# Another layout of the slots in which a DeltaNet mixer emits its work

## The chip, the cores and the metric

The kernel runs on one core of one Trainium2 chip. A core has five engines that run side by side and wait for each other on semaphores: TensorE (PE, matrix products; its weight loads are shown apart as PEld), VectorE (DVE), ScalarE (ACT), GpSimd (POOL) and SyncE (SP, which here only starts transfers). Transfers between the core's memory and the chip's main memory are made by 16 DMA engines. Each engine takes its instructions in one fixed order. The metric is the device time of one execution in microseconds; less is better.

## The reference, cut to what matters

One inference step of a small trunk of two layers on 128 context tokens and 512 latent tokens of width 1024. Layer 0 mixes tokens with a gated DeltaNet, layer 1 with a long convolution (Hyena); each is followed by a SwiGLU feed-forward. The change concerns the DeltaNet mixer alone.

```python
def _gdn_mixer(h, w_in, conv_w, a_log, dt_bias, onorm, w_out, s0):
    proj = h @ w_in
    qkv = jax.nn.silu(_dwconv(proj[..., :GDN_CONV_W], conv_w)).astype(f32)
    q = _l2norm(...) * GDN_DK ** -0.5
    k = _l2norm(...)
    v = ...
    gate = proj[..., GDN_CONV_W:GDN_CONV_W + GDN_V_W]...
    o_f, s_f = _chunk_gated_delta(q, k, v, g[:, :, 0], beta[:, :, 0], s0[:, 0])
    o_b, s_b = _chunk_gated_delta(rev(q), rev(k), rev(v), ...)
    o = o_f + rev(o_b)
    o = (o * lax.rsqrt(jnp.mean(o * o, axis=-1, keepdims=True) + EPS)
         * onorm.astype(f32) * jax.nn.silu(gate))
    return o.reshape(...) @ w_out, jnp.stack([s_f, s_b], axis=1)
```

Inside `_chunk_gated_delta`, chunks of 64 tokens are prepared independently of each other (a triangular system is solved for each), and then a scan over the chunks carries a 128x128 state: two chunks for the context, eight for the latent tokens, in both directions.

## The kernel before

All 640 tokens lie together, features on the partitions. Dense products are made with each operand split into a high and a low part (three matmuls of 320 columns for each block of 128 features), so one head's projection of one kind is 2 halves x 8 blocks x 3 = 48 matmuls.

The mixer (`gdn`) is written as generators that yield after each part of their work. For each head there are these streams:

- `gemm` (`gdn_gemm`, L940 and after), one for each of q, k and v (numbers 0, 1, 2; `GEMM_ORDER` takes k first): a 512 KB weight load, its split on ACT and DVE, 48 matmuls `ps_p` in 9 parts, copies to `xp`. `conv` (`gdn_conv`) follows: the short convolution, five steps of 0.9 us on DVE and ACT, in 6 parts.
- `pre` (`gdn_pre` and `gdn_norms`, L979 to L1122), 18 parts: transposes, sums of squares on ACT, a reciprocal root on DVE, `fa` (L1053), then a trip through main memory. The ACT queue sends `fa` out (`ft`, L1060) and brings 16x16 blocks back (`ln`, L1067); DVE negates them into `bn` (L1073, L1074) and solves small triangular systems in many short operations. The results go out and back again (L1112, L1119) as `tm` and `tt`.
- `chunks` (`gdn_chunks`, L1125 to L1184), 11 parts: the rest of the solve, 50 matmuls of 64 to 128 columns (`ps_c`, `ps_aq`, `ps_y`), and the transposed v in `vyz`.
- `scan` (`gdn_scan`, L1187 to L1262), 30 parts, ten steps: PE `ps_s` (L1214), DVE `y` (L1219), PE (L1225 or L1227), ACT `w` or `od` (L1233), PE (L1248), DVE `s` (L1254), for both directions side by side.
- `norm` (`gdn_norm`), 4 parts: the output's norm and its transpose. `gate` (`gdn_gate`), 9 parts: the gate's projection, 48 matmuls `ps_gate` with a weight load and a split like those of `gemm`; its result is stored to main memory. `finish` (`gdn_finish`): a finished head is loaded, multiplied by its gate where that was not done yet, and split into the high and low parts (`xh`, `xl`, L316, L317) that the output product `ps_o` reads.
- `loads`: parts of `ada` (L192 to L226), the products that give the modulation of later sublayers. Two parts make one step: two 512 KB loads and four matmuls `ps_ada` of 32 rows, each in its own quarter of the array. There are 64 parts, that is 32 steps, in the mixer.

The loop over heads has 11 iterations, h from -3 to 7. Iteration h emits the scan of head h, the chunks of head h+1, the preparation of head h+2, the projections and convolutions of head h+3 and the norm of head h-1. So the first three iterations fill the pipeline (the ramp), in h = 5, 6, 7 the projections have run out, and at h = 7 the loop drains. Each iteration has 30 slots, and `weave` walks through them: in slot t a stream with n parts and slots (a, b) emits parts until n(t+1-a)/(b-a) are out. Within one slot the streams come in the order of `EMIT`.

```python
        for t in range(slots):
            for st in live:
                g, n, a, b, done = st
                while st[4] < min(n, n * (t + 1 - a) / (b - a)):
                    next(g, None)
                    st[4] += 1
```

`PERIOD` holds the slots of the streams that every head has; where it has three entries, the first is for the ramp, the second for h = 0 to 4, the third for h = 5 and later. `GATES[g]` gives the iteration and the slots of gate g. `LOADS[h+3]` gives the number of `ada` parts of iteration h and their slots. The framework below then orders the instructions of each engine: an instruction that is emitted earlier goes first where both are ready by the framework's own estimate of times. So the place of a part is a rank, not a fixed time.

Weight loads and `ada` loads share five buffers (`raw`) and the SP queue. The DMAs of `ft` and `ln` go by the ACT queue.

Of the kernel before, what the change touches and what calls it, by code (L numbers as in the profile page):

```python
# [33 lines left out]
SLOTS = 30  # L34
PERIOD = dict(
    scan=(0, SLOTS),
    norm=(11, 21),
    pre=((2, 21), (1, 25), (4, 25)),
    chunks=((7, 30), (1, 25), (3, 20)),
    gemm=((2, 8, 14), (0, 10, 20), (22, 0, 11)),  # L40
    gemm_len=(8, 7, 10),
    finish=(27, 30),
)
GEMM_ORDER = (1, 0, 2)

GATES = (
    (5, 15, 25),
    (-3, 17, 20),
    (6, 16, 24),
    (4, 5, 14),  # L50
    (4, 13, 28),
    (3, 23, 30),
    (7, 27, 30),
    (7, 3, 15),
)

LOADS = (
    (0, 0, 28),
    (3, 10, 26),
    (0, 5, 30),  # L60
    (10, 3, 26),
    (3, 1, 22),
    (1, 7, 29),
    (3, 6, 30),
    (6, 0, 26),
    (13, 0, 21),
    (18, 0, 24),
    (11, 5, 30),
)

EMIT = ['scan', 'loads', 'norm', 'conv', 'chunks', 'pre', 'gemm', 'finish', 'gate']
MOD_PARTS = (4, 5, 4, 1, 1, 0, 1, 3, 4)
HALVES = (slice(0, 320), slice(320, 640))
DIAG = 128 * 128 + 128
# [13 lines left out]
class _Kernel:  # L88
# [624 lines left out]
    def gdn(self, xs):  # L713
        nc, A, V, G, PE, I = self.nc, self.A, self.V, self.G, self.PE, self.I
        W = I["gdn_w_in"][0]
        with ExitStack() as st:
# [78 lines left out]
            for h in range(-3, H):  # L795
# [3 lines left out]
                def add(name, stream, n, slots):  # L799
                    streams.append((EMIT.index(name), stream, n, *slots))  # L800

# [887 lines left out]
```

## Time and profile before

| | us |
|---|---|
| three runs | 2103.25, 2105.75, 2108.15; median 2105.75 |
| the profiled execution's own time | 2103.4 |
| its span in the profile | 2101.6 |
| PE busy in the span | 2033.6 (97%) |
| DVE, ACT, POOL busy | 1260.7, 794.1, 135.6 |
| granted TensorE clock, mean | 0.989 |
| mixer, first projection matmul to first matmul of the output product | 135.1 to 715.1 |

The span runs from the first to the last instruction of the profile. "Busy" of PE is the time in which at least one matmul is under way; matmuls overlap, and their ends are modelled, so a busy PE may still have room. The granted clock is the share of full speed that TensorE's throttle let through. The ramp lies at 135 to 268 us, and the iterations h = 0 to 7 begin, by the second part of each scan, at about 268, 310, 371, 424, 482, 556, 615 and 677 us; the last scan ends at 714.

### The profile page before, as it was taken

The page shows a single profiled execution, that of the slowest core. Times are in us where ns is not written, and L with a number is a line of the kernel's source. Part 1 is how long each engine was busy: PE and PEld are TensorE (multiplying, and loading weights), DVE is VectorE, ACT ScalarE, POOL GpSimd, SP SyncE. Part 2 cuts the span into 40 slices and gives each one's busy share as a digit, 9 for nine tenths or more (in the row PEclk, how much of TensorE's full clock was granted, in tenths as well). Part 3 has the DMA queues.
Part 4 walks back from the last instruction along what each step waited for, and adds up shares of the span by engine and source line. Part 5 has one row for each costly group of instructions (what it writes and reads, how often), then busy time and mean ns, then how long its engine had stood idle before and what let it go on. Part 6 is the DMA issues. An engine that isn't in the chain of part 4 may idle for free.

```text
span 2101.6 us, 34710 instructions
## 1 busy us (share of the span) xinstructions
PE 2033.6 (97%) x13779; PEld 1889.1 (90%) x13779; DVE 1260.7 (60%) x2649; ACT 794.1 (38%) x1761; POOL 135.6 (6%) x241
## 2 busy tenths in 40 slices
PE   7998999999989999999999999999999999999997
PEld 4677888988866899999999999999889999999997
DVE  6887887876654464434434467878775443443444
ACT  4456445555533443212222243333344321221222
POOL 0131011110110100000000001010000000000000
PEclk8999999999989999999999999999999999999998
DMA  7856453344555632222222253222453222222221
GB/s 236 274 184 154 113 153 100 83 124 115 183 180 181 200 119 62 79 81 70 72 81 71 58 162 100 82 85 76 141 161 95 72 81 71 71 81 71 71 63 58
DMA packets 344833, 237.01 MB, mean 113 GB/s; under 512 B 62274, under 2 KB 314810, under 8 KB 344671
## 3 DMA queue, kind: packets, MB, share of 16 engines
q1 hardware_dynamic: 322495, 230.18, 36.7%
q10 hardware_dynamic: 22176, 4.62, 1.1%
q8 instruction: 108, 1.77, 0.4%
q14 instruction: 54, 0.44, 0.1%
HBM read 202.57 MB, written 32.19 MB: 112 GB/s over the span
## 4 chain that ended last, share of the span: by engine, by line
PE 81%; DVE 7%; ACT 4%; DMA 3%; issue 2%; POOL 0%; ACTq 0%; POOLq 0%; DVEq 0%
PE ps_g L131 15%; PE ps_u L131 15%; PE ps_d L131 15%; PE ps_hp L143 8%; PE ps_o L131 5%; PE ps_p L143 4%; PE ps_ada L209 2%; PE ps_ab L1467 2%; PE ps_g L1524 2%; PE ps_gate L143 1%; PE ps_s L1248 1%; PE ps_s L1214 1%; PE ps_y L1161 1%; PE ps_s L1225 1%; DMA ft<-fa 1%
## 5 line engine op out<-in xcount | busy, mean ns | idle before, releaser
L118 ACT CAST wh<-raw 128x1024 fp32r<-128x1024 f32 (+2 forms) x241 | 220.8, 921 | 461.3 <-PE ps_d L131 199.3
L119 DVE TENSOR_TENSOR wl<-raw,wh 128x1024 fp32r<-128x1024 f32 (+2 forms) x241 | 257.2, 1071 | 79.1 <-ACT wh L118 78.1
L131 PE MATMUL ps_g<-fh,wh 128*128 128x320 f32 (+1 forms) x704 | 220.2, 313 | 0.0
L131 PE MATMUL ps_g<-fh,wl 128*128 128x320 f32 (+1 forms) x704 | 219.6, 312 | 0.0
L131 PE MATMUL ps_u<-fh,wh 128*128 128x320 f32 (+1 forms) x704 | 219.5, 312 | 0.0
L131 PE MATMUL ps_u<-fh,wl 128*128 128x320 f32 (+1 forms) x704 | 219.4, 312 | 0.0
L131 PE MATMUL ps_g<-fl,wh 128*128 128x320 f32 (+1 forms) x704 | 218.0, 310 | 0.0
L131 PE MATMUL ps_u<-fl,wh 128*128 128x320 f32 (+1 forms) x704 | 217.9, 310 | 0.0
L416 DVE SCALAR_TENSOR_TENSOR x<-ps_d,mod,x 128x128 f32<-128x128 f32 x144 | 58.8, 437 | 154.0 <-PE ps_d L131 153.9
L131 PEld LDWEIGHTS ps_g<-fl,wh 128*128 128x128 f32 x704 | 133.6, 190 | 0.4 <-DVE fl L308 0.2
L131 PEld LDWEIGHTS ps_g<-fh,wh 128*128 128x128 f32 x704 | 133.5, 190 | 0.3 <-ACT fh L307 0.2
L131 PEld LDWEIGHTS ps_u<-fh,wh 128*128 128x128 f32 x704 | 133.6, 190 | 0.0
L131 PEld LDWEIGHTS ps_u<-fl,wh 128*128 128x128 f32 x704 | 133.4, 190 | 0.0
L131 PEld LDWEIGHTS ps_u<-fh,wl 128*128 128x128 f32 x704 | 132.8, 189 | 0.0
L131 PEld LDWEIGHTS ps_g<-fh,wl 128*128 128x128 f32 x704 | 132.5, 188 | 0.0
L143 PE MATMUL ps_p<-xh,wh 128*128 128x320 f32 x384 | 128.4, 334 | 1.8 <-ACT junk L1000 0.9
L143 PE MATMUL ps_hp<-xh,wh 128*128 128x322 f32 (+1 forms) x384 | 123.0, 321 | 0.7 <-DVE xp L1415 0.7
L143 PE MATMUL ps_p<-xh,wl 128*128 128x320 f32 x384 | 122.5, 319 | 0.0
L143 PE MATMUL ps_p<-xl,wh 128*128 128x320 f32 x384 | 122.2, 318 | 0.0
L143 PE MATMUL ps_hp<-xh,wl 128*128 128x320 f32 (+1 forms) x384 | 119.5, 311 | 0.0
L143 PE MATMUL ps_hp<-xl,wh 128*128 128x320 f32 (+1 forms) x384 | 119.4, 311 | 0.0
L131 PE MATMUL ps_d<-xh,wl 128*128 128x320 f32 x384 | 118.8, 309 | 0.0
(376 smaller groups left out, 5110.7 us busy)
## 6 DMA issues: line engine op xcount, KB each, us to landing
raw<-in_ada_w_dram SPq DMA_DIRECT2D x96, 512.0 KB
raw<-in_ffn_w_gu_dram SPq DMA_DIRECT2D x88, 512.0 KB
raw<-in_gdn_w_in_dram SPq DMA_DIRECT2D x33, 512.0 KB
raw<-in_ffn_w_down_dram SPq DMA_DIRECT2D x32, 512.0 KB
raw<-in_hy_w_in_dram SPq DMA_DIRECT2D x24, 512.0 KB
h_lat<-hlo SPq DMA_DIRECT2D x16, 512.0 KB
hs<-h_lat SPq DMA_DIRECT2D x32, 256.0 KB
raw<-in_ffn_w_down_dram SPq DMA_DIRECT2D x16, 384.0 KB
```

The source lines that it names most:

```text
L118: self.A.copy(wh[:, ks, :], v[:, ks])
L119: self.V.tensor_sub(wl[:, ks, :], v[:, ks], wh[:, ks, :])
L131: self.PE.matmul(ps, a[:, k, :], b[:, sl], start=(n == 0), stop=(n == 3 * nk - 1))
L143: self.PE.matmul(ps, a[:, k, :], b[:, sl], start=(n == 0), stop=(n == 3 * nk - 1))
L209: PE.matmul(ps[32 * j : 32 * j + 32, :], self.sc[:, k, :], loaded[j * 512 // n][:, c : c + 512], start=(k == 0), stop=(k == KD - 1), skip_ ...
L416: V.scalar_tensor_tensor(out=x[d][:, sl], in0=p1[:, pl], scalar=gate[:, c, d : d + 1], in1=x[d][:, sl], op0=ALU.mult, op1=ALU.add)
L1161: PE.matmul(ps[:, n : n + 128], tm[:, d, t, :], cur[:, d, t, :], start=True, stop=True)
L1214: PE.matmul(pss[d][:, 0:128], qk[:, t, c * 128 : c * 128 + 128], state[seq, d], start=True, stop=True)
L1225: PE.matmul(p2, lt[:, d, t, c, :], ys[d], start=True, stop=True)
L1248: PE.matmul(pss[d][:, 256:384], ktok[:, t, c, :], ws[d], start=True, stop=True)
L1467: PE.matmul(ps, a_[:, m, it, js], b_[it], start=(c == 0), stop=(c == 5))
L1524: PE.matmul(pv[:, gi * 256 : gi * 256 + 256], a_[:, e, cs], b_[:, m, jt, :], start=(c == 0), stop=(c == 11))
```

## The change

Only constants change. No instruction is added to the program or taken from it; the streams are emitted in other slots, and in another order within a slot.

```diff
 PERIOD = dict(
     scan=(0, SLOTS),
-    norm=(11, 21),
-    pre=((2, 21), (1, 25), (4, 25)),
+    norm=(12, 19),
+    pre=((2, 21), (0, 24), (0, 25)),
     chunks=((7, 30), (1, 25), (3, 20)),
-    gemm=((2, 8, 14), (0, 10, 20), (22, 0, 11)),
-    gemm_len=(8, 7, 10),
-    finish=(27, 30),
+    gemm=((1, 8, 14), (0, 10, 20), (22, 1, 11)),
+    gemm_len=(4, 7, 8),
+    finish=(26, 30),
 )
 GATES = (
-    (5, 15, 25),
-    (-3, 17, 20),
+    (5, 15, 24),
+    (-3, 17, 19),
     (6, 16, 24),
-    (4, 5, 14),
+    (4, 6, 11),
     (4, 13, 28),
-    (3, 23, 30),
-    (7, 27, 30),
-    (7, 3, 15),
+    (3, 21, 30),
+    (7, 26, 30),
+    (6, 3, 9),
 )
 LOADS = (
     (0, 0, 28),
-    (3, 10, 26),
-    (0, 5, 30),
-    (10, 3, 26),
-    (3, 1, 22),
-    (1, 7, 29),
-    (3, 6, 30),
-    (6, 0, 26),
-    (13, 0, 21),
-    (18, 0, 24),
-    (11, 5, 30),
+    (4, 5, 30),
+    (0, 5, 29),
+    (10, 3, 28),
+    (3, 1, 19),
+    (1, 6, 29),
+    (2, 5, 25),
+    (6, 2, 28),
+    (16, 1, 21),
+    (18, 0, 23),
+    (8, 5, 30),
 )
-EMIT = ['scan', 'loads', 'norm', 'conv', 'chunks', 'pre', 'gemm', 'finish', 'gate']
+EMIT = ['finish', 'scan', 'norm', 'conv', 'chunks', 'loads', 'pre', 'gemm', 'gate']
```

Worked through `weave`, this is what moves:

- In the ramp a projection's nine parts take 4 slots instead of 8, and its convolution begins 4 or 5 slots earlier.
- In h = 0 to 4 the preparation begins at slot 0 instead of 1 and ends a slot earlier; projections and chunks stay where they were. The norm is a slot later. Gate 3 is packed into slots 6 to 10 of h = 4, gate 5 is spread over slots 21 to 29 of h = 3.
- In h = 5 the preparation of head 7, the last one, begins at slot 0 instead of 4.
- Gate 7 goes from slots 3 to 13 of h = 7 to slots 3 to 8 of h = 6.
- h = 5 gets 16 `ada` parts instead of 13, h = 7 gets 8 instead of 11; h = -2 gets one more and h = 3 one less.
- `finish` starts at slot 26 instead of 27 of h = 7 and comes first in its slots; gate 6 also starts at 26.
- Within a slot, `loads` come after norm, convolution and chunks instead of ahead of them.

## The prediction

> **What bounds the kernel now.** I read the page first. Its rows give the span, each engine's busy time, and the engines' shares of the chain that ended last.
>
> ```profile
> span 2101.6 us, 34710 instructions
> ...
> PE 2033.6 (97%) x13779; PEld 1889.1 (90%) x13779; DVE 1260.7 (60%) x2649; ACT 794.1 (38%) x1761; POOL 135.6 (6%) x241
> ...
> PE 81%; DVE 7%; ACT 4%; DMA 3%; issue 2%; POOL 0%; ACTq 0%; POOLq 0%; DVEq 0%
> ```
>
> PE is the bound, and the change removes no matmul. It can only win time in which PE idles, runs at a lower clock, or works at poor density. So I asked the windows view for the ramp, the eight iterations and the end (cut at the first L1225 or L1227 matmul of each head). Columns: window, its length, busy us (and count) of PE, PEld, DVE, ACT, POOL, then granted clock, DMA share, GB/s.
>
> ```profile
> 135.00:268.00 133.00, 121.00 (x859) 104.47 (x861) 103.33 (x216) 77.97 (x203) 24.06 (x60) 1.00 0.52 139
> 268.00:310.00 42.00, 41.02 (x327) 35.71 (x327) 35.13 (x91) 17.98 (x52) 6.27 (x16) 1.00 0.55 150
> 310.00:371.00 61.00, 59.86 (x482) 53.51 (x480) 46.86 (x127) 36.74 (x117) 10.79 (x21) 1.00 0.43 112
> 371.00:424.00 53.00, 50.91 (x425) 47.68 (x423) 43.66 (x122) 30.23 (x101) 9.53 (x21) 1.00 0.32 84
> 424.00:482.00 58.00, 55.77 (x448) 49.62 (x448) 44.03 (x123) 31.72 (x107) 9.85 (x21) 1.00 0.44 118
> 482.00:556.00 74.00, 70.31 (x566) 65.22 (x566) 47.51 (x123) 34.69 (x113) 7.57 (x18) 1.00 0.48 139
> 556.00:615.00 59.00, 54.96 (x413) 40.39 (x415) 39.26 (x118) 27.82 (x94) 8.05 (x12) 0.97 0.54 167
> 615.00:677.00 62.00, 58.28 (x362) 40.48 (x354) 24.09 (x67) 20.74 (x62) 4.53 (x10) 0.89 0.66 207
> 677.00:714.00 37.00, 36.91 (x245) 28.64 (x245) 18.57 (x56) 19.73 (x59) 6.07 (x10) 1.00 0.68 199
> 714.00:740.00 26.00, 22.10 (x125) 20.45 (x124) 13.00 (x33) 13.06 (x35) 1.55 (x2) 0.87 0.48 153
> ```
>
> Length less PE busy is the idle time: 12.0 in the ramp, then 1.0, 1.1, 2.1, 2.2, 3.7, 4.0, 3.7 and 0.1 for h = 0 to 7, and 3.9 at the end; 33.9 in all. The clock costs (1 - clock) times length: 1.8 in h = 5, 6.8 in h = 6, 3.4 at the end; 12.0 in all. So 46 us is the most that any layout could win. Smaller windows show where the loss of h = 6 and of the end sits, in the same columns:
>
> ```profile
> 617.00:622.00 5.00, 2.01 (x14) 0.91 (x12) 2.09 (x12) 4.79 (x16) 0.00 (x0) 1.00 0.94 262
> 623.00:637.00 14.00, 13.59 (x64) 9.99 (x63) 3.23 (x7) 3.19 (x10) 0.00 (x0) 0.51 0.50 180
> 719.00:726.00 7.00, 6.57 (x26) 6.57 (x27) 4.53 (x15) 3.63 (x10) 0.00 (x0) 0.53 0.72 225
> ```
>
> After 3 us of idle between 617 and 622 the clock stays at 0.51 for 14 us; 64 matmuls in 14 us is half the density of the other windows. Where do the projections and gates lie? The windows view of `ps_gate` alone (PE, PEld, ACT, clock, DMA) and that of `ps_ada`:
>
> ```profile
> 556.00:615.00 59.00, 10.64 (x48) 7.82 (x48) 0.88 (x2) 0.97 0.54 167
> 615.00:677.00 62.00, 9.53 (x52) 7.63 (x52) 0.87 (x2) 0.89 0.66 207
> 677.00:714.00 37.00, 21.37 (x87) 13.55 (x87) 0.87 (x2) 1.00 0.68 199
> ```
> ```profile
> 556.00:615.00 59.00, 13.12 (x63) 1.92 (x66) 0.59 (x1) 0.97 0.54 167
> 615.00:677.00 62.00, 16.20 (x62) 2.05 (x54) 0.59 (x1) 0.89 0.66 207
> 677.00:714.00 37.00, 7.38 (x32) 1.02 (x32) 0.59 (x1) 1.00 0.68 199
> ```
>
> Iteration 7 has 87 of the gates' matmuls in 37 us and no idle PE; iteration 6 has 52 in 62 us, and the cold stretch. The timeline gives the stalls themselves (start, length, what, and in brackets the idle time before it and who ended it):
>
> ```profile
> 599.81 0.28 DVE L1073 TENSOR_SCALAR bn<-ln 40x256 f32<-40x256 f32 x1 [2.06 <-DMA ln<-ft]
> 601.43 0.37 DVE L1074 TENSOR_SCALAR bn<-ln 40x256 f32<-40x256 f32 x1 [1.33 <-DMA ln<-ft]
> ```
> ```profile
> 603.24 0.80 PE L1214 MATMUL ps_s<-s,qk 128*128 128x128 f32 x2 [3.71 <-DVE s L1254]
> ...
> 718.47 0.44 PE L131 MATMUL ps_o<-xh,wh 128*128 128x320 f32 x1 [2.31 <-ACT xh L316]
> ...
> 719.43 0.63 PE L131 MATMUL ps_o<-xh,wh 128*128 128x320 f32 x1 [0.52 <-ACT gt L1308]
> ```
>
> The longest PE gap, 3.71 us, is named after DVE's `s`, but DVE itself stood at `bn`, waiting for the small blocks of head 7 to come back from memory; `s` was queued behind. The gap at 718 waits for ACT to split the finished heads.
>
> **The change, part by part.** The prices come from the chain of waits (start, length, what): pieces of the mixer, and one group of 24 matmuls of 320 columns.
>
> ```profile
> 586.95 7.22 DMA ft<-fa
> 594.66 6.75 DMA ln<-ft
> ...
> 612.97 0.99 PE ps_ada L209 x8
> ...
> 637.86 0.97 PE ps_ada L209 x2
> 639.25 0.97 PE ps_ada L209 x2
> 640.65 0.98 PE ps_ada L209 x4
> ...
> 701.65 0.49 PE ps_gate L143 x2
> ...
> 710.08 1.25 ACT xh L316 x2
> ```
> ```profile
> 2026.69 3.58 PE ps_g L131 x24
> ```
>
> A matmul is 3.58/24 = 149 ns, a gate of 48 is 7.2 us. An `ada` step has 8 records: 0.99 us when the four products stay together.
>
> *h = 7* loses gate 7 (7.2) and three `ada` parts, 1.5 steps of 7.38/4 = 1.85 us: 2.8. With PE busy 36.91 of 37, the bound is -10.0 if PE alone sets the pace, and 0 if the scan's own chain through DVE and ACT does. Busy is not full, PEld has 28.64 of 37, so I take -6. What is late next is gate 6, emitted at slots 26 to 29; its matmuls ran well ahead of those (701.65 is two thirds into the iteration), so it fills the gaps.
>
> *h = 6* receives the gate: one 512 KB load on SP past its `ada` loads, the split on ACT and DVE (ACT has 20.74 busy of 62, DVE 24.09, so both cover it), 48 matmuls at slots 3 to 8, 621 to 634 by the old times: the cold stretch. Ends: +7.2 if PE only gets more to do, and +7.2 - 6.8 - 3.7 = -3.3 if idle and cold both vanish. The load and the split come before the first matmul, so I take half of the 10.5: +2.0.
>
> *h = 5*: the preparation of head 7 moves four slots, 4 x 59/30 = 7.9 us. Its `ft` would leave at 579 instead of 587 and `ln` be back at 593.5 instead of 601.4. DVE would wait for it as before, but gate 0 is emitted at slots 15 to 23 (585 to 602) and would now cover it. Ends: -5.5 (the 3.7 and the cold 1.8) and 0; I take -4. Three `ada` parts more are 1.5 steps of 13.12/(63/8) = 1.67: +2.5. Together -1.5. The preparation's matmuls, ACT squares and the two transfers on the ACT queue pass only the start of scan 5; a later `y` or `w` is bounded by the same 3.7.
>
> *The end*: `finish` starts a slot earlier (37/30 = 1.2 us) and ahead of the scan. Six splits of ACT are already queued at 716 to 719, where PE waits 2.31. Ends: -6.2 (2.3, 0.5 and the cold 3.4) and +3.7, six ACT splits of 1.25/2 ahead of the last `w`; I take -1, near the slot that moves.
>
> *Ramp and h = 0 to 4*: the packing of the projections, the preparation one slot earlier, the norm one later, gates 3 and 5, the single loads that move. PE idles 22.1 us here. The layout may close or open gaps of the kind that are there: ends -11 (half of them) and +8. No row says which, so 0. Cover: the projections keep PE busy at full clock throughout.
>
> Sum: -6 + 2 - 1.5 - 1 + 0 = -6.5. The profiled execution took 2103.4 (1.8 outside its span), which gives 2096.9; the median of the runs is 2.35 higher, which gives 2099.3. I name 2098.
>
> [...]
>
> **The rivals.**
>
> *The gate only moves (no change).* PE is busy 58.28 of 62 us in h = 6 too; if that is real work, +7.2 and +2.5 there and in h = 5 take back the 10 of h = 7: about 2103.5. The same comes out if the framework's order hardly follows the slots: gate 6 already ran ten slots ahead of its place. Against it: the clock of 0.89.
>
> *The end goes cold (no change).* With gate 7 gone, h = 7 may idle and meet what happened at 623: 6.8 us lost, 2103.4 - 6.5 + 6.8 = 2103.7. Against it: gate 6 and the first `ps_o` are left to fill.
>
> *Broken `ada` steps (slower).* `loads` now rank behind norm, convolution and chunks of the same slot, so that a chunk's matmuls can come between the four products of a step. A step in one piece took 0.99; in three pieces 0.97 + 0.97 + 0.98. Each break costs about 1 us. h = 5 to 7 hold 42 parts, 21 steps: from 7 breaks more the gain is gone, from 11 the kernel is slower by over 0.2%; 16 more give 2098 + 16 = 2114. For it: the rows at 637 to 641. Against it: chunks fell between them in the old order too.
>
> **How the numbers follow.** The forecast gets 0.58, the gate that only moves 0.17, the cold end 0.08, the broken steps 0.17. A measurement tells about 0.2%, 4.2 us, from no change: below 2101.5 is faster (0.58), to 2110 the same (0.25), above it slower (0.17). The forecast's own range is 2082 to 2104: -10 for h = 7, -3.3 for h = 6, -3 for h = 5 and some of the rest at one side, the rival without a gain at the other. To hold 8 in 10 I go down to 2080, half of the ramp's end with it, and up to 2111, into the broken steps.
>
> **What would show it.** Right: h = 7 at about 31 us, no cold stretch near 623 or a shorter one, `bn` of head 7 some 8 us earlier without a PE gap behind it. Wrong: h = 6 longer by 7 and as cold as before, `ps_ada` busy well above 1.7 us a step, a granted clock below 0.9 in h = 7, or a ramp that differs by more than 5 us, which I left at 0.

## The result, and the profile after

| | before | after |
|---|---|---|
| median, us | 2106.26 (2103.25 to 2108.15) | 2070.75 (2069.52 to 2072.83) |
| ratio, 95% interval | | 0.9834 [0.9817, 0.9851] |
| profiled execution, us | 2103.4 | 2071.53 |
| its span | 2101.6 | 2069.7 |

The change makes the kernel 1.7% faster: 35.5 us between the medians of four runs each, 31.9 between the two spans. The forecast was 2098, its range went down to 2080, so 2070.75 lies below it. The page after, the rows that answer to those of before:

```profile
span 2069.7 us, 34716 instructions
...
PE 2012.0 (97%) x13779; PEld 1882.6 (91%) x13779; DVE 1261.2 (61%) x2649; ACT 792.7 (38%) x1761; POOL 135.4 (7%) x241
...
PE 84%; DVE 6%; ACT 4%; DMA 4%; issue 1%; POOL 1%; SPq 0%; ACTq 0%; POOLq 0%; DVEq 0%
```

PE has the same 13779 matmuls, and yet is busy 21.6 us less. So most of the gain isn't idle time; it is the same matmuls, under way for less time. The windows view after, cut as before (window, length, busy us and count of PE, PEld, DVE, ACT, POOL, granted clock, DMA share, GB/s):

```profile
135.00:267.00 132.00, 124.82 (x875) 107.74 (x873) 103.73 (x216) 80.70 (x210) 25.30 (x61) 0.99 0.55 149
267.00:317.00 50.00, 49.33 (x388) 42.99 (x388) 41.67 (x107) 23.77 (x68) 10.26 (x21) 1.00 0.59 162
...
485.00:556.00 71.00, 68.89 (x551) 60.97 (x550) 47.08 (x124) 34.87 (x117) 7.50 (x15) 1.00 0.47 138
556.00:604.00 48.00, 46.56 (x369) 35.03 (x368) 33.59 (x105) 21.11 (x73) 5.85 (x10) 1.00 0.72 222
604.00:657.00 53.00, 52.46 (x422) 41.62 (x418) 23.17 (x67) 20.61 (x63) 4.55 (x10) 1.00 0.79 259
657.00:692.00 35.00, 33.49 (x233) 29.43 (x230) 22.97 (x60) 23.67 (x65) 5.25 (x10) 1.00 0.71 213
692.00:718.00 26.00, 22.21 (x132) 21.15 (x131) 16.60 (x45) 13.76 (x37) 1.00 (x2) 0.87 0.37 119
```

No iteration has a cold stretch any more: the clock of h = 6 went from 0.89 to 1.00, and the end alone still has 0.87. Iteration 6 holds more matmuls in less time.

These windows are cut at the first scan matmuls, some of which are missing from a trace, so their borders can be a few us off. A surer mark is ACT's first copy of the context state (L1257) in each scan. The timeline before, heads 0, 5, 6, 7, and after:

```profile
275.52 0.26 ACT L1257 COPY s<-ps_s 128x128 f32<-128x128 f32 x1
...
569.83 0.26 ACT L1257 COPY s<-ps_s 128x128 f32<-128x128 f32 x1
...
625.88 0.27 ACT L1257 COPY s<-ps_s 128x128 f32<-128x128 f32 x1
...
684.89 0.27 ACT L1257 COPY s<-ps_s 128x128 f32<-128x128 f32 x1
```
```profile
270.52 0.27 ACT L1257 COPY s<-ps_s 128x128 f32<-128x128 f32 x1 [0.58 <-PE ps_s L1248]
...
563.13 0.26 ACT L1257 COPY s<-ps_s 128x128 f32<-128x128 f32 x1
...
613.56 0.26 ACT L1257 COPY s<-ps_s 128x128 f32<-128x128 f32 x1
...
666.32 0.27 ACT L1257 COPY s<-ps_s 128x128 f32<-128x128 f32 x1
```

With the last L1225 of the scans at 714.0 and 691.8, the 31.9 us come from: 5.0 up to head 0, 1.7 from there to head 5, 5.6 from head 5 to head 6 (56.0 to 50.4), 6.2 from head 6 to head 7 (59.0 to 52.8), 3.6 from there to the last scan's end (29.1 to 25.5), and 9.7 behind it.

**Three sources.** The windows view of `ps_ada` alone over the whole mixer, the kernel before and the kernel after (PE, PEld, ACT, clock, DMA):

```profile
135.00:760.00 625.00, 59.20 (x256) 8.21 (x256) 2.35 (x4) 0.98 0.51 145
```
```profile
135.00:760.00 625.00, 46.15 (x256) 6.77 (x256) 2.32 (x4) 0.99 0.52 150
```

The same 256 records, 32 steps of 8, keep PE busy 59.20 us before and 46.15 after: 13.1 us. The steps are cut into fewer pieces by other matmuls: in PE's timeline the records stand in 54 pieces before, 13 of them whole steps of 8, and in 42 after, 20 of them whole. That is 1.1 us for each piece less, and over the 20 kernels profiled for this document (42 to 55 pieces) a straight line of 1.08 us for each piece gives the `ada` time to within 1.5 us. From head 6 to head 7 the same view says, before and after:

```profile
625.90:684.90 59.00, 16.65 (x60) 2.21 (x60) 0.59 (x1) 0.91 0.59 193
```
```profile
613.50:666.30 52.80, 10.63 (x72) 1.55 (x72) 1.16 (x2) 1.00 0.79 256
```

12 records more in 6 us less. The second source is idle time of PE: length less busy, summed over windows cut at the marks, is 33.9 us before and 23.2 after. The third is the clock, (1 - clock) times length: 11.5 and 4.7 (the clock is given to 0.01, so this is good to about 1.5 us). 13.1 + 10.7 + 6.8 = 30.6 of the 31.9, though some `ada` records at half clock before (1.9 us of them) count in two of the terms. The windows show one execution of each kernel. The granted clocks of all runs agree with it: (1 - clock) times span is 23.7 to 25.6 us on average in five sets of runs of the kernel before, and 17.1 in the four after.

**Where the cold stretch was.** It began at the border of scans 5 and 6. The timeline of PE, ACT and DVE before (start, length, what, and in brackets the idle time before it and who ended it):

```profile
616.72 1.04 PE L209 MATMUL ps_ada<-raw,sc 128*32 128x512 f32 x2
619.05 0.49 PE L1225 MATMUL ps_s<-y,lt 128*128 128x128 f32 x2 [1.28 <-DVE y L1219]
620.53 0.45 PE L1138 MATMUL ps_c<-tm,fa 64*64 64x64 f32 x8 [1.00 <-ACT vyz L1182]
...
618.23 3.01 ACT L1182 ACTIVATE vyz<-ps_vt,rinv 64x128 f32<-64x128 f32 x8
...
618.24 0.17 DVE L1269 SCALAR_TENSOR_TENSOR om<-oss,eq 128x5 f32<-128x5 f32 x1 [2.71 <-ACT junk L1244]
...
618.64 0.35 DVE L1219 SCALAR_TENSOR_TENSOR y<-ps_s,sy,vyz 128x128 f32<-128x128 f32 x1
```

DVE stands 2.71 us at the norm of head 5 (`om`), which waits for ACT's sums of squares; `y` of the scan is queued behind it, ACT then copies `vyz` for 3 us, and PE has nothing left but two records of a torn `ada` step. After the change the same border looks like this:

```profile
605.42 1.06 PE L209 MATMUL ps_ada<-raw,sc 128*32 128x512 f32 x6
606.41 0.41 PE L143 MATMUL ps_gate<-xh,wh 128*128 128x320 f32 x1
...
607.84 0.31 PE L143 MATMUL ps_gate<-xh,wh 128*128 128x320 f32 x1
...
607.46 1.87 ACT L1182 ACTIVATE vyz<-ps_vt,rinv 64x128 f32<-64x128 f32 x5
...
607.47 0.17 DVE L1269 SCALAR_TENSOR_TENSOR om<-oss,eq 128x5 f32<-128x5 f32 x1 [2.98 <-ACT junk L1244]
```

DVE's wait is still there, 2.98 us, and so is ACT's work. What differs is that PE has gate 7's matmuls to do meanwhile. The stall wasn't removed; it was covered.

**The end.** The windows view of `ps_o` alone, after, and before:

```profile
670.00:680.00 10.00, 1.73 (x8) 1.21 (x8) 0.00 (x0) 0.00 (x0) 1.00 0.56 179
680.00:690.00 10.00, 7.66 (x36) 5.31 (x37) 0.00 (x0) 0.00 (x0) 1.00 0.69 219
```
```profile
700.00:710.00 10.00, 0.00 (x0) 0.00 (x0) 0.00 (x0) 0.00 (x0) 1.00 1.05 294
```

51 matmuls of the output product run under scan 7 (44 of them in these windows), where gate 7 and 24 records of `ada` were (after the change none is left there). At 149 ns each that is 7.6 of the 9.7 us won behind the last scan.

### The profile page after: what moved, and what is told of

The parts are those of the page before. It is cut to its first block, busy times and chain, and to the rows that moved or that the text cites. A ratio compares the mean times of both kernels' runs of the same rounds, so it can differ in the third digit from the quotient of the medians.

```text
span 2069.7 us, 34716 instructions
## 1 busy us (share of the span) xinstructions
PE 2012.0 (97%) x13779; PEld 1882.6 (91%) x13779; DVE 1261.2 (61%) x2649; ACT 792.7 (38%) x1761; POOL 135.4 (7%) x241
## 4 chain that ended last, share of the span: by engine, by line
PE 84%; DVE 6%; ACT 4%; DMA 4%; issue 1%; POOL 1%; SPq 0%; ACTq 0%; POOLq 0%; DVEq 0%
PE ps_g L131 15%; PE ps_u L131 15%; PE ps_d L131 15%; PE ps_hp L143 8%; PE ps_o L131 6%; PE ps_p L143 5%; PE ps_ab L1467 2%; PE ps_g L1524 2%; PE ps_ada L209 2%; PE ps_gate L143 2%; PE ps_s L1248 2%; PE ps_y L1161 2%; PE ps_s L1214 1%; DMA raw<-in_gdn_w_in_dram 1%; PE ps_s L1225 1%
```

## The experiments

All are medians of several runs beside runs of the kernel before. "us" is (1 - ratio) x 2105. The last four columns are of the profiled execution, against the kernel before's 59.2, 33.9, 11.5 and 2101.6: PE time of the 256 `ada` records, idle time and clock loss in the mixer, and the span. The changes of the three add up to that of the span within 4 us in every kernel but that with gate 7 alone (-16.8 against -8.4; what grew there is not shown). Each is one execution, and a few us of a column can be chance: in the ramp, which they share, the kernel before idles 12.8 us, that with gate 7 alone 13.5, and that with the preparation of head 7 alone 11.7.

| kernel | median | ratio, 95% interval | us | ada | idle | clock | span |
|---|---|---|---|---|---|---|---|
| order within a slot alone | 2102.57 | 0.9992 [0.9978, 1.0005] | -1.7 | 57.4 | 32.3 | 14.5 | 2101.0 |
| preparation of head 7 alone | 2093.83 | 0.9954 [0.9937, 0.9970] | -9.7 | 58.2 | 28.3 | 6.7 | 2090.6 |
| gate 7 alone | 2091.65 | 0.9945 [0.9927, 0.9963] | -11.6 | 54.0 | 30.7 | 3.1 | 2093.2 |
| late ada parts alone | 2091.56 | 0.9941 [0.9923, 0.9959] | -12.4 | 53.9 | 32.6 | 1.4 | 2086.2 |
| all late edits | 2085.69 | 0.9912 [0.9897, 0.9927] | -18.5 | 49.8 | 31.3 | 4.8 | 2084.1 |
| all early edits | 2091.30 | 0.9944 [0.9926, 0.9962] | -11.8 | 56.6 | 27.9 | 13.2 | 2094.9 |
| - packed ramp alone | 2102.61 | 0.9989 [0.9972, 1.0006] | -2.3 | 55.4 | 33.7 | 15.0 | 2098.6 |
| - early without the ramp | 2094.89 | 0.9958 [0.9943, 0.9972] | -8.8 | 57.9 | 26.8 | 11.8 | 2094.3 |
| - - preparation alone | 2097.66 | 0.9967 [0.9955, 0.9979] | -6.9 | 58.0 | 28.5 | 15.1 | 2099.7 |
| - - norm, gates 3 and 5 | 2103.38 | 0.9993 [0.9979, 1.0007] | -1.5 | 59.7 | 33.3 | 15.9 | 2104.7 |
| - - early ada parts | 2101.54 | 0.9991 [0.9981, 1.0002] | -1.9 | 56.5 | 32.9 | 10.0 | 2100.0 |
| after | 2070.75 | 0.9834 [0.9817, 0.9851] | -34.9 | 46.2 | 23.2 | 4.7 | 2069.7 |
| after, old order in a slot | 2071.32 | 0.9842 [0.9820, 0.9864] | -33.3 | 46.7 | 23.6 | 1.8 | 2069.2 |
| after, old preparation of head 7 | 2076.12 | 0.9866 [0.9849, 0.9882] | -28.2 | 47.1 | 28.6 | 5.2 | 2075.9 |
| after, gate 7 back in h = 7 | 2074.55 | 0.9862 [0.9847, 0.9878] | -29.0 | 51.1 | 23.6 | 0.0 | 2071.4 |
| after, old late ada parts | 2077.90 | 0.9873 [0.9850, 0.9896] | -26.7 | 51.5 | 22.2 | 2.7 | 2076.9 |
| after, more ada parts moved | 2073.84 | 0.9857 [0.9841, 0.9873] | -30.1 | 47.4 | 23.6 | 3.4 | 2071.1 |
| before, gate stored by ACT's queue | 2103.33 | 0.9985 [0.9975, 0.9996] | -3.2 | 60.6 | 35.4 | 10.1 | 2101.3 |
| after, gate stored by ACT's queue | 2084.69 | 0.9892 [0.9866, 0.9919] | -22.7 | 50.0 | 29.6 | 5.1 | 2082.0 |

### One late edit at a time

```diff
-EMIT = ['scan', 'loads', 'norm', 'conv', 'chunks', 'pre', 'gemm', 'finish', 'gate']
+EMIT = ['finish', 'scan', 'norm', 'conv', 'chunks', 'loads', 'pre', 'gemm', 'gate']
```

> The kernel before with the new order within a slot alone (finish first, loads behind norm, convolution and chunks). Theory A, density: the matmuls of a modulation step (ps_ada) stay together because its loads rank behind the chunks, and each break saved is worth 1 us of PE; from h = 5 on the pieces fall from 34 towards 20, and the time falls by 8 to 12 us. Theory B, the last head's dates: the gain comes from the early preparation of head 7, so this run stays within 4 us of before. Theory C, cover: the gain comes from the gate moved into h = 6 and the loads, so this run stays within 4 us of before and keeps the cold stretch near 623.

Measured: nothing that can be told from no change, and 57.4 us of `ada`, in 33 pieces from h = 5 on where the kernel before has 34. The place of `loads` within a slot neither breaks nor mends the steps.

```diff
-    pre=((2, 21), (1, 25), (4, 25)),
+    pre=((2, 21), (1, 25), (0, 25)),
```

> The kernel before with the preparation of head 7 from slot 0 of h = 5 instead of 4, nothing else. Theory B: fa of head 7 comes some 8 to 10 us earlier, the PE gap of 3.7 us and its cold clock go, h = 5 shortens by 5 to 11 us, the time falls by 8 to 15 us. Theories A and C: the time stays within 4 us of before, since the pieces of ps_ada and the place of the gate are as they were.

Measured: 9.7 us faster. The idle time falls by 5.6 and the clock loss by 4.8; `ada` stays at 58.2. This one acts through the stall of the last preparation.

```diff
-    (7, 3, 15),
+    (6, 3, 9),
```

> The kernel before with gate 7 at slots 3 to 8 of h = 6 instead of 3 to 13 of h = 7, nothing else. Theory C: the 48 matmuls fill the cold stretch of h = 6, the clock there rises from 0.89 to above 0.95, and output matmuls take the gate's place under scan 7; the time falls by 8 to 15 us. Theories A and B: the gate only moves, 0 to 4 us less.

Measured: 11.6 us faster, with gap and all: PE still has an idle stretch of 3.70 at 608.7. But the clock loss falls from 11.5 to 3.1, and `ada` from 59.2 to 54.0.

```diff
-    (13, 0, 21),
-    (18, 0, 24),
-    (11, 5, 30),
+    (16, 1, 21),
+    (18, 0, 23),
+    (8, 5, 30),
```

> The kernel before with 16, 18, 8 modulation parts in h = 5, 6, 7 instead of 13, 18, 11, nothing else. Theory C: three parts less in h = 7 let the end come earlier by about 3 us, and h = 5 gets longer by about 2.5: within 4 us of before. Theories A and B: within 4 us of before too; were it more than 8 us, none of the three would hold.

Measured: 12.4 us faster, the largest of the four, where all three theories had said within 4, and that above 8 none of them would hold. What they left out is that the new numbers of parts also change how the steps are cut: `ada` falls to 53.9, and there is no cold stretch in h = 5 to 7, though gate 7 is still in h = 7.

### The late edits together, the early ones together, and one taken back

The first of these kernels is the one before with the four diffs above and the lines of the change for gates 0 and 6 and `finish`:

```diff
-    finish=(27, 30),
+    finish=(26, 30),
-    (5, 15, 25),
+    (5, 15, 24),
-    (7, 27, 30),
+    (7, 26, 30),
```

The second is the changed kernel with all of these undone, which leaves the edits of the ramp and of h = 0 to 4 (and the norm's, which holds in every iteration).

> The kernel before with every edit that acts from h = 5 on (preparation of head 7, gate 7, gate 0, loads of h = 5 to 7, finish, gate 6, the order within a slot); ramp and h = 0 to 4 keep the old slots. Three of these edits alone gave -11 to -14 us each. Theory A, sum: they pay apart, so together -30 us or more and the early slots are worth nothing. Theory B, one loss: they remove the same stall and cold stretch between h = 5 and h = 6, and apart from it only the end gains, so together -20 to -28 us, and the early slots give the rest of the 35.

> The kernel before with the new slots of the ramp and of h = 0 to 4 alone (projections packed, preparation from slot 0, norm, gates 1, 3 and 5, loads up to h = 4); from h = 5 on, and the order within a slot, as before. Theory A: within 4 us of before. Theory B: head 5's first context state comes 5 to 8 us earlier than in the kernel before (569.8 us), as it does in the changed kernel (563.1), and the time falls by 5 to 12 us.

Measured: 18.5 and 11.8. The three late edits alone add up to 33.7, together they give 18.5, so they take away one loss in common; 18.5 is less than either theory of the first kernel had it (20 to 28, or 30 and more). The columns say which loss. The clock can be won once: 4.8, 8.4 and 10.1 us alone, 6.7 together; by the mean clock of all their runs 8.7, 11.3 and 9.7 alone, 7.0 together. The `ada` time adds up: 1.0, 5.2 and 5.3 alone, 9.4 together. And 18.5 + 11.8 = 30.3 against 34.9 for the whole change: with intervals of 3 to 4 us on each, late and early edits add, as far as this can tell.

The other two are the changed kernel with one edit undone:

```diff
-    pre=((2, 21), (0, 24), (0, 25)),
+    pre=((2, 21), (0, 24), (4, 25)),
```

> The changed kernel with the preparation of head 7 back at slot 4 of h = 5. Theory A: 8 to 14 us slower than the changed kernel (2070.75). Theory B: the gate and the loads cover for it, 0 to 4 us slower.

```diff
-    (6, 3, 9),
+    (7, 3, 15),
```

> The changed kernel with gate 7 back at slots 3 to 13 of h = 7. Theory A: 10 to 16 us slower than the changed kernel (2070.75). Theory B: the part of the gate that is the stretch in h = 6 is covered by the others, but the output matmuls that ran under scan 7 (51 in the changed kernel, 7.6 us) go back behind it: 6 to 9 us slower.

Measured: 5.4 and 3.8 us slower than the changed kernel by the medians, 6.7 and 5.9 by the ratios. The first lies between its two theories, the second under both. Without the early preparation the idle time is back (28.6 against 23.2; 3.0 of the 5.4 lies between heads 5 and 6, the rest where the two layouts are alike), `ada` stays whole and the clock is hardly touched. Without gate 7 in h = 6, `ada` is back at 51.1, but nothing goes cold: the clock loss is 0.0. What covers the border of scans 5 and 6 there? Its timeline of PE, and of DVE:

```profile
605.40 1.90 PE L209 MATMUL ps_ada<-raw,sc 128*32 128x512 f32 x10
...
607.81 0.79 PE L1138 MATMUL ps_c<-tm,fa 64*64 64x64 f32 x18
...
608.22 0.17 DVE L1269 SCALAR_TENSOR_TENSOR om<-oss,eq 128x5 f32<-128x5 f32 x1 [4.05 <-ACT junk L1244]
```

Ten records of `ada` and the first chunk products take the gate's place, while DVE waits even longer. So work other than the gate's covers it too; two records of a torn step, as before, did not.

### The rest of the late edits, and one step further

These are the changed kernel with the first diff of this section undone (`EMIT`), and with the fourth undone (`ada` parts 13, 18, 11).

> The changed kernel with the old order within a slot. Theory A: the order is worth nothing in either layout (it measured -0.8 of 2105 us with the old slots): within 3 us of the changed kernel, 2068 to 2074, and some 50 output matmuls still run under scan 7, because gate 7 has left it. Theory B: the order pays once the slots are new, by finish in front: 2076 to 2081, with under 20 output matmuls under scan 7.

> The changed kernel with the old numbers of ada parts in h = 5 to 7 (13, 18, 11). Theory A (one shared loss, which the other two late edits remove without this one): 2072 to 2077. Theory B (separate gains: 13 us with the old layout): 2080 to 2084. Theory C: three parts more for h = 7 meet an iteration that the gate has left, and cost nothing: 2068 to 2072.

Measured: 0.6 and 7.2 us slower. The order is worth nothing in the new layout either: 51 output matmuls still run under scan 7, so it isn't `finish` in front that lets them. Nor is it the departure of gate 7 by itself: with gate 7 moved and the old `ada` parts only 8 run there (in the kernel with gate 7 alone and in the second one here), and with the new `ada` parts and gate 7 back 10. It takes both to make room. The `ada` parts cost a little more than the first theory allowed and less than the second: 51.5 us of `ada`, no cold stretch. Taking back any of the three late edits costs less than that edit wins alone, and the clock column says why: without it the cold stretch behind the border stays away, since the other two are there.

```diff
-    (16, 1, 21),
+    (18, 1, 21),
     (18, 0, 23),
-    (8, 5, 30),
+    (6, 5, 30),
```

> The changed kernel with 18 ada parts in h = 5 and 6 in h = 7 (16 and 8 there), an attempt to go on in the direction that paid: taking three parts back measured 7.2 us slower. Theory A: what is gained is idle time and the cold stretch, and the change has removed both (h = 5 to 7 idle 3.9 us at a clock of 1.00): within 3 us of the changed kernel. Theory B: each part moved out of h = 7 is worth 2.4 us: 4 to 5 us faster.

Measured: 2073.84, 3.1 us above the changed kernel; no gain. `ada` is at 47.4, and there is nothing left to cover. The attempt doesn't beat the change.

### Which early edit

The packed ramp by itself, then all early edits without it:

```diff
-    gemm=((2, 8, 14), (0, 10, 20), (22, 0, 11)),
-    gemm_len=(8, 7, 10),
+    gemm=((1, 8, 14), (0, 10, 20), (22, 0, 11)),
+    gemm_len=(4, 7, 10),
```

> The kernel before with the packed projections of the ramp alone (nine parts in 4 slots instead of 8). The early edits together measured 13.3 us faster. Theory A: they win in the ramp, where PE idles 12.0 us and only 7.2 after the change: this one is 8 to 13 us faster, head 0's first state copy moves from 275.5 to 270-273. Theory B: the win comes from h = 0 to 4: this one is within 3 us of before.

> The kernel before with the early edits but without the packed ramp: preparation a slot earlier and norm a slot later in h = 0 to 4, gates 3 and 5, the single loads that move. Theory A (the ramp wins): within 4 us of before. Theory B (h = 0 to 4 win): 8 to 13 us faster, the ramp as before and the interval from head 0's to head 5's first state copy 294.3 us in the kernel before, at most 288 here. If the cases are separate, this and the packed ramp add up to 13.3.

Measured: 2.3 (not told from no change) and 8.8, so the early gain lies in h = 0 to 4 and not in the ramp; there it takes 290.6 us from head 0 to head 5, less than the 294.3 before but more than the 288 expected. In the profile of the packed ramp head 0's first copy comes at 268.2, 7.3 us earlier than before; the last scan ends at 712.9, only 1.1 earlier. At head 5 it is still ahead by 4.9. Most of what it loses then lies at the border of scans 5 and 6, as the windows view of that kernel's iteration 6 shows:

```profile
605.55:672.83 67.28, 63.58 (x370) 42.53 (x369) 26.90 (x72) 21.07 (x62) 5.23 (x10) 0.85 0.60 187
```

The clock is 0.85 over 67 us: in this execution the cold stretch grew. Over its ten runs the mean clock loss is only 1.1 us above that of the kernel before, so the rest isn't explained, and whether the packed ramp keeps its lead beside the late edits was not run.

Three kernels split the second, except for the slot of gate 1, which is in none of them. In this diff, a blank line stands between them:

```diff
-    pre=((2, 21), (1, 25), (4, 25)),
+    pre=((2, 21), (0, 24), (4, 25)),

-    norm=(11, 21),
+    norm=(12, 19),
-    (4, 5, 14),
+    (4, 6, 11),
-    (3, 23, 30),
+    (3, 21, 30),

-    (3, 10, 26),
+    (4, 5, 30),
-    (0, 5, 30),
+    (0, 5, 29),
-    (10, 3, 26),
+    (10, 3, 28),
-    (3, 1, 22),
+    (3, 1, 19),
-    (1, 7, 29),
+    (1, 6, 29),
-    (3, 6, 30),
+    (2, 5, 25),
-    (6, 0, 26),
+    (6, 2, 28),
```

> The kernel before with the preparation of h = 0 to 4 at slots 0 to 23 instead of 1 to 24, nothing else. The early edits without the packed ramp measured 10.4 us faster. Theory A: the preparation carries it, since it starts the trip through main memory earlier: 7 to 11 us faster. Theory B: the ada parts and gates that lie beside the heads carry it: within 3 us of before.

> The kernel before with the norm at slots 12 to 18 instead of 11 to 20 and gates 3 and 5 at their new slots in h = 4 and 3, nothing else. Theory A (the preparation carries the 10.4 us): within 3 us of before. Theory B (gates): 4 to 10 us faster, gate 5 being spread over h = 3. Theory C: the norm, which DVE reaches at the border of two scans and at which y queues (2.71 us of waiting at 618 in the kernel before), gives it: the wait ahead of om under 1 us at that border, and 3 to 7 us faster.

> The kernel before with the ada parts of h = -2 to 4 at their new slots and numbers (one more in h = -2, one less in h = 3), nothing else. Theory A (the preparation): within 3 us of before. Theory B (filler placement): 4 to 10 us faster. If the three single cases add up to 10.4 they win in different places, if to more they remove one loss.

Measured: 6.9, and 1.5 and 1.9, which can't be told from nothing. Their sum of 10.3 is about the 8.8 of all. The norm's later slot does nothing at the border of scans 5 and 6: DVE waits the same 2.71 us there. One slot's start of the preparation carries the gain. How is less sure: its idle time up to head 5 is 18.4 us against 22.3, but its profiled execution is one of the longer ones (2101.46 where the median is 2097.66), reaches head 5 no earlier than the kernel before (570.1 and 569.8), and shows little more.

### Is it the queue?

The waits of SP's queue from head 5's mark to the last scan's end (for whom, us in total, times, longest), in the kernel before, and in the kernel after:

```profile
SPq L200 <- PE ps_ada L209: 49.3, 10, 9.5
SPq L1309 <- ACT gt L1308: 17.8, 3, 13.6
```
```profile
SPq L200 <- PE ps_ada L209: 45.2, 12, 12.9
SPq L1309 <- ACT gt L1308: 5.4, 2, 4.4
```

In the kernel before SP stands 13.6 us at the store of a gate's result (from 595.4 to 609.0), with the next `ada` loads behind it, which leave from 619.4 on. A theory suggests itself: starved of loads, PE has torn steps and no work at the border. One line takes that store off SP:

```diff
-        self.nc.sync.dma_start(self.g_dram[h], sg)
+        self.nc.scalar.dma_start(self.g_dram[h], sg)
```

> The kernel before with one line changed: a gate's result is stored to main memory by the ACT queue instead of SP's. SP stood 13.6 us at such a store between 595 and 609 (17.8 us at three of them from h = 5 on), with the ada loads of the next steps queued behind it. Theory A: this starves PE of ada work, so that ada steps are torn and nothing is left for the border of scans 5 and 6: 5 to 12 us faster, the granted clock of h = 6 at 1.00, and under 28 pieces of ada from h = 5 on (34 in the kernel before). Theory B: the loads wait for free buffers anyway: within 3 us of before.

> The changed kernel with the same one line, an attempt to beat it. SP waits 5.4 us at gate stores there from h = 5 on, and 45.2 us for ada buffers, so its loads run ahead. Theory A: nothing is starved any more, within 3 us of the changed kernel, 2068 to 2074. Theory B: SP's waits still cost in the ramp and in h = 0 to 4: 3 to 8 us faster.

Measured: 3.2 us faster on the kernel before, 13.9 slower (medians) on the changed one. The theory falls as it was put: `ada` stays at 60.6, in 33 pieces from h = 5 on, and the clock loss is 10.1. SP's waits in that kernel say why the load doesn't come sooner:

```profile
SPq L1261 <- DVE rr_t L174: 13.7, 1, 13.7
SPq L1112 <- DVE zz L1102: 12.1, 1, 12.1
```

The wait has gone over to the next instruction in the queue, the results of head 7's solve (L1112): 12.1 us, which end at 613 as before. In the changed kernel the line moves work everywhere: the mark of head 2 comes 8.7 us later, `ada` is back at 50.0, idle time at 29.6. One line, which moves the eight gates' stores, gives a new order on all engines (PE's differs from 193 us on, the first of these stores leaves at 188), and it costs four tenths of what the layout had won.

## Why the prediction was wrong

The sign and the list of places were right: a cold stretch that the gate fills, a stall behind the last preparation, an end with room in it. The sizes were not, by a factor of five, and nearly all of them to the same side. The steps that failed are terms of the sum: density, which got no term (13.1 us), h = 6 (+2.0 against -6.2), the ramp and h = 0 to 4, put at 0 without a row (-6.7), and the end (-1 against -9.7).

- **"46 us is the most that any layout could win."** Wrong as a bound. It counts idle time and clock. The third source, named in the sentence before it as poor density, was left out of the sum: 13.1 us of `ada`. Of the 46, the change won 17.5 (10.7 and 6.8).
- **Broken `ada` steps, the rival on the slow side.** The mechanism exists (54 pieces before, 42 after), and so does its price (1.1 us a piece); the direction was the opposite. I looked at the rank of `loads` within a slot, which is worth nothing (0.9992). Gate 7's place and the numbers of parts each mend steps worth 5 us (54.0 and 53.9 from 59.2). The steps of before were already torn, and I took their mean, 1.67 and 1.85 us a step, for a price of the work: from head 6 to head 7 it was 16.65/(60/8) = 2.2 before and 10.63/(72/8) = 1.2 after.
- **h = 6, "I take half of the 10.5: +2.0".** Measured -6.2, below its lower end of -3.3. By the windows the idle time falls from 3.7 to 0.5 and the cold stretch is gone, and the `ada` work, 12 records more, takes 6 us less. The 48 matmuls of the gate stand in time that PE otherwise spends waiting or at half clock.
- **h = 5, -1.5.** Measured -5.6. The early preparation did what was said, row and all:

```profile
586.16 0.29 DVE L1073 TENSOR_SCALAR bn<-ln 40x256 f32<-40x256 f32 x1 [0.24 <-DMA ln<-ft]
```

  DVE waits 0.24 instead of 2.06, 13.7 us earlier (6.7 of it because head 5 itself begins earlier), and no PE gap follows. I had 8 us and a DVE wait of the old size. The +2.5 for three more `ada` parts was 0.9 (9.50 to 10.37 us of `ada` from head 5 to head 6).
- **h = 7, -6, and the end, -1.** Measured -3.6 and -9.7. Here the mechanism was seen and put in the wrong place: "gate 6 and the first `ps_o` are left to fill", I wrote of h = 7. They do fill it, so it gets shorter by less, and the 7.6 us of output work done there come off the end. `finish` a slot earlier is not enough: with gate 7 back, 10 output matmuls run there.
- **Ramp and h = 0 to 4, "No row says which, so 0".** Measured -6.7 at head 5's mark, and 11.8 for these edits alone. The preparation is the main part. It is the same move, by one slot instead of four, that I priced at -4 for head 7; here it got 0, since no single stall of 3.7 us stood there, only 10.1 us of small gaps (1.0 to 3.7 in each iteration).
- **"The gate only moves"** (0.17) falls: h = 6 takes the gate and gets shorter. (Its support was misread: gate 6 ran not ten slots ahead but some seven, its first matmul at 701.6, slot 20 of 30, its first part emitted in slot 27.) **"The end goes cold"** (0.08) falls for h = 7; the end keeps its 0.87.

The cold stretch behind the border stands in other kernels too. In the one with the store on ACT's queue:

```profile
620.00:624.80 4.80, 2.06 (x30) 1.88 (x30) 2.57 (x12) 2.49 (x9) 0.02 (x1) 0.79 1.06 355
625.00:637.00 12.00, 12.00 (x57) 8.87 (x58) 2.13 (x5) 3.70 (x11) 0.00 (x0) 0.52 0.43 159
637.00:641.00 4.00, 4.00 (x18) 1.54 (x16) 0.70 (x2) 0.31 (x2) 0.00 (x0) 1.00 0.23 47
```

PE is busy for all of 12 us and still at 0.52. Before it lie 4.8 us with PE busy for 2.06, as in the kernel before 5 us with 2.01. After the full gap of 3.71 us in the kernel before, behind which 320-column matmuls of a gate follow, the clock is 0.66 from 602 to 607 and 1.00 from 607 to 612, which is about 3.4 us at half clock (0.34 x 5 / 0.5); behind the border, where chunk products of 64 to 128 columns follow, it is 14 (0.51 from 623 to 637). What makes the difference isn't shown. In the changed kernel the gate runs during the stall, not behind it, and no cold stretch begins (1.00 from 604 to 612, PE busy for 7.73 of 8 us); that is why "half" was too little. Whether the gate right behind the border would have cut the stretch short was not run.

What stays open is why the steps become whole. The order of PE is fixed when the kernel is built, and gate 7's place and the numbers of parts both change it so that more steps stay whole. Moving the stores off SP changes it too, but mends no step: 55 pieces where the kernel before has 54, and 47 where the changed kernel has 42. Which estimate of the framework cuts a step into 2 and 6 records was not found. How the earlier preparation wins its 7 us in h = 0 to 4 is open too; its idle time (22.3 to 18.4) is the only hint.

## What to carry to other kernels

Price a moved piece of work by its whole form (0.99 us for an `ada` step in one piece), not by the mean of a trace that holds it in pieces; the difference between the two, times the count, is a gain that neither idle time nor clock shows. Where a stall recurs at every border of two stages, look for what PE can do during it: work that is free to move belongs at the uncovered border; here the gate's matmuls served (clock 1.00 from 604 to 612), and `ada` with chunk products did too (1.00 from 600 to 610 with gate 7 back). Edits that each cure the same loss didn't add here (33.7 us for three late edits one by one, 18.5 for all late edits together), so make them together and undo them one by one before believing any of their single prices.

## What the hardware showed

- An `ada` step's four products run side by side (four of its records are under way at 612.9 before, each 592 to 617 ns long). In these rows a part of a step kept PE busy as long as a whole one: 1.04 us for 2 records (616.72 before), 1.06 for 6 (605.42 after), 1.06 for 8 (612.90 before), and 0.99 for 8 in the rows of the prediction.
- Three times a stretch of about 5 us in which PE was busy for some 2 was followed by 12 to 14 us at half clock, though PE was busy nearly throughout: in the kernel before (2.01 of 5.00, then 14 us, busy 13.59 at 0.51), with the store on ACT's queue (2.06 of 4.80, then 12, busy 12.00 at 0.52), and with the early edits without the ramp (2.26 of 5.00 from 608 to 613, then 12, busy 11.59 at 0.50). In the kernel before, no single gap of that stretch was longer than 1.28 us.
- The mixer's stretches at half clock, by the clock records of the two traces: in the kernel before 3.4 us from 602.6, 13.7 from 623.1 and 6.8 from 718.6; in the kernel after 3.4 from 151.2 and 6.8 from 697.3.
- Moving the gate's store to another queue didn't free the queue it left: 13.6 us at that store became 12.1 us at another store, that of head 7's solve (L1112). It gained little in the kernel before (0.9985 [0.9975, 0.9996]), and with it the changed kernel takes 0.7% longer (2084.69 against 2070.75), beside a new order on all engines.
